# One masked product over 128 rows in a gated recurrence, and its operations ordered behind the weight splits of their steps

## The chip, the cores and the metric

The kernel runs on one core of a Trainium2 chip. The metric is the time of one execution on the device in microseconds. A profile is a trace of one execution, with each engine's instructions: TensorE (PE, with its weight loads PEld), VectorE (DVE), ScalarE (ACT), GpSimd (POOL), SyncE (SP) and the DMA queues.

## What is computed

The reference is two layers of a decoder trunk over 256 tokens of width 2048. Layer 0 has a mixer with two halves: chunked spatial gating (A) and a gated linear recurrence with 8 heads of width 128 (B). Layer 1 has an attention with 16 heads. Each layer ends in a gated MLP with a short convolution. Only the recurrence of half B is touched by the change:

```
k = (1 - lb) * sigmoid(-f);   log_f = log(lb + (1 - lb) * sigmoid(f))
per head, per chunk of 64 tokens, with G = cumsum(log_f):
  o_t = (q_t * exp(G_t)) @ state  +  sum over s <= t of (q_t * exp(G_t - G_s) . k_s) * i_s
  state = exp(G_end) * state + sum over s of (k_s * exp(G_end - G_s)) outer i_s
o = rms_norm(o) * silu(g)
```

Everything else of the trunk is large projections: a 256 x 2048 activation times weight matrices that add up to 435 MB.

## The kernel before

**The projections.** The weights stream from memory once, in pieces of 512 KB (128 partitions by 1024 floats). `weights` loads a piece `w` through SP's queue and splits it in `halves` (lines 187 to 190) into a rounded high half `wh` by ACT (line 188) and a low half `wl` by DVE (line 189). TensorE then multiplies high by high, high by low and low by high, so that three matmuls in a lower precision stand for one in full precision. `project_four`, `project_tok` and `project` differ in which side is moved; their matmuls are lines 363 to 365, 344 to 346 and 319. One piece is one *step*: the projection calls `tick()`, then `weights`, then writes out the step's matmuls, 12 of 512 columns or 24 of 256. There are four buffers for `w` and three each for `wh` and `wl`.

**Side work.** Everything that isn't a projection is written as Python generators. `tick()` advances up to `depth[0]` of them by one `yield`, so that their operations are written out between the pieces. A planner then fixes the order on each engine: it keeps the dependencies and, where an operation that was written earlier isn't ready by its own model of time, puts a later one that is ready ahead of it. On the chip each engine follows that order. Two helpers bind the planner. `tied` keeps a matmul behind the projection matmul written last. `held` (with the anchor "wh" by default, or "wl") adds an order without a semaphore: the operation may not stand ahead of the split that was written last, the `wh` split on ACT or the `wl` split on DVE.

```
def held(r, last="wh"):

    tc.add_manual_dep(r.ins, deep[last].ins.name, order, reason="not before")
```

**The gates** (`gates`, lines 671 to 688). For two groups of four heads, six steps after their projection: four sigmoids on ACT give the forget gates `l` and the two key tiles in `t` (lines 679 to 682; the trace puts them on line 100, in the helper `act`), and DVE scales the keys (line 685). Only the first sigmoid of a head is held.

**The recurrence** (`hgrn`, lines 716 to 818). A head starts at least `PACE` = 4 steps after the head before, and goes by `yield`s:
- Step 1: ACT turns `l` into the decay (line 723). DVE inverts a half of it into `kd` (line 727), ACT copies keys into `kd` (line 728), POOL multiplies them (lines 729 and 731) and forms the running products `tot` of the levels 2 to 64 (line 737).
- Step 2: eight small matmuls (line 742) of 32 rows and 32 columns each give the pairs of neighbouring tokens, two for each of the four 32-row blocks. Their results lie in one PSUM tile `dg`, 128 rows by 2 x 32 columns. Then DVE multiplies them with the mask `two` into the diagonal blocks of the state tile `st` (128 rows by 2 x 128 columns): four products of 32 rows by 64 elements, one for each block (line 745).
- Steps 3 to 5: seven levels; for each, ACT copies two halves into `E` (line 757), and DVE multiplies queries and keys with the decay (line 761, or 764 at the last one).
- Five steps on: the matmuls of the levels (lines 771 and 779), ACT's copies (lines 782 and 784), DVE's five masked copies into `st[:, 1]` (line 790), and ACT's copy to `s1` (line 793).
- Some five steps on: the output matmuls with the values (lines 801 to 803) and their evacuation (lines 805 and 809).

`sts` are four state tiles that the heads take in turn. They are set to zero once (line 709); only the blocks that line 745 writes, and the places that lines 784 and 790 write, change afterwards.

While the eight heads go through, the projections of the queries (`project`, line 864), of the values (`project_tok`, line 823) and of the output gate (`project_four`, line 869) run on TensorE.

Of the kernel before, what the change touches and what calls it, by code (L numbers as in the profile page):

```python
# [12 lines left out]
ALU = mybir.AluOpType  # L13
# [42 lines left out]
def tile_trunk(ctx: ExitStack, tc: tile.TileContext, x, pp_d, cst_d, mlev_d, msk_d,  # L56
# [36 lines left out]
    def act(out_, in_, func, **kw):  # L93
        name = TABLE.get(func)
        if name is not None and name != epoch["set"]:
            ld = SC.preload_act_table_set(name)
            for o in epoch["ops"]:
                tc.add_manual_dep(ld.ins, o.ins.name, order, reason="table order")
            epoch.update(set=name, load=ld, ops=[ld])
        r = SC.activation(out_, in_, func, **kw)  # L100
        if name is not None:
            tc.add_manual_dep(r.ins, epoch["load"].ins.name, order, reason="table order")
            epoch["ops"].append(r)
        return r
# [403 lines left out]
    def mixer_ab(norm):  # L508
# [162 lines left out]
        def gates(j, z):  # L671

            for _ in range(LAG):
                yield
            for i in range(4):
                l = keep("lf")
                t = hp.tile([P, 4, P], F32, tag="two", name=nm("kq"), bufs=2 * NH)
                first, second = view(z, i * S, (2, P)), view(z, (i + 1) * S - 1, (-2, P))
                held(act(l[:, 0:P], first, AF.Sigmoid))
                act(l[:, P:S], second, AF.Sigmoid)  # L680
                act(t[:, 0], first, AF.Sigmoid, scale=-1.0)
                act(t[:, 3], second, AF.Sigmoid, scale=-1.0)
                h = len(kq)
                ks = view(t, 0, (3 * P, 2), (1, P))
                V.tensor_scalar(ks, ks, omlb[:, h:h + 1], None, ALU.mult)
                lf.append(l)
                kq.append(t)
                yield
# [16 lines left out]

        H = P // 2
        sts = [hp.tile([P, 2, P], F32, tag=f"st{i}", name=f"st{i}") for i in range(4)]
        for st in sts:
            V.memset(st, 0.0)

        within = [px.tile([P, 512], F32, tag=f"lv{i}", name=f"lv{i}") for i in range(2)]
        for w in within:
# [3 lines left out]
        def hgrn(h):  # L716
# [3 lines left out]
                yield  # L720
            first[0] = steps[0] + PACE
            yield
            SC.activation(l, l, AF.Identity, bias=lb[:, h:h + 1], scale=omlb[:, h:h + 1])
            st = sts[h % 4]
            kd = hp.tile([P, 2, P], F32, tag="kd", name=nm("kd"), bufs=1)
            later, kb = view(l, 1, (P - 1, 2), (2, H)), view(kd, 1, (P - 1, 2), (2, H))
            V.reciprocal(kb, later)
            SC.activation(view(kd, 0, (P + 1, 2), (2, H)), view(t, 0, (3 * P + 1, 2), (2, H)), AF.Copy)
            nc.gpsimd.tensor_tensor(kb, kb, view(t, 1, (3 * P - 1, 2), (2, H)), ALU.mult)
            qs = view(t, 2 * P + 1, (-P - 1, 2), (2, H))  # L730
# [9 lines left out]
            for T in range(2):  # L740
                for r in range(0, P, BLK):
                    tied(PE.matmul(dg[r:r + BLK, T * BLK:(T + 1) * BLK], kd[:, T, r:r + BLK], t[:, 2 - T, r:r + BLK],
                                   start=True, stop=True))
            for r in range(0, P, BLK):
                V.tensor_tensor(st[r:r + BLK, :, r:r + BLK], dg[r:r + BLK, 0:2 * BLK].rearrange("p (a b) -> p a b", a=2),
                                two[r:r + BLK, :, r:r + BLK], ALU.mult)
            yield

            qs = view(t, 2 * P, (1 - P, 2), (2, H))
            V.tensor_tensor(qs, qs, view(l, 0, (P + 1, 2), (2, H)), ALU.mult)  # L750
            E = hp.tile([P, NL - 1, 2, P], F32, tag="E", name=nm("E"), bufs=2)
            for li in reversed(range(NL)):
                n = LEVELS[li]
                m = P // n
                for sl in range(2 if n > 1 else 0):
                    to = P + n if sl else 3 * P + n
                    SC.activation(E[:, li, sl].rearrange("p (b two n) -> p b two n", two=2, n=n),
                                  view(t, P * sl, (2 * n, 64 // n), (to, 2), (1, n)), AF.Copy)
                if li:
                    both = view(t, 0, (2 * P + n, 2), (2 * n, P // n), (1, n))  # L760
                    V.tensor_tensor(both, both, view(tot[n], 1, (-1, 2), (2, m), (0, n)), ALU.mult)  # L761
                else:
                    even = view(t, 0, (P, 2), (1, n))
                    V.tensor_tensor(even, even, view(tot[n], 1, (m, 2), (0, n)), ALU.mult)
                if n in (4, 16):
                    yield
# [12 lines left out]
                    deep["last"] = tied(PE.matmul(d[r:r + BLK, c:c + n], E[:, li, 0, r:r + BLK], E[:, li, 1, o:o + n],  # L779
                                                  start=True, stop=True))  # L780
            s128 = hp.tile([P, P], F32, tag="s128", name=nm("s128"), bufs=3)
            SC.activation(back(s128), xps[:, 0:P], AF.Copy)
            for r in (0, H):
                SC.activation(st[r:r + H, r // H, H - r:P - r], xps[r:r + H, P:P + H], AF.Copy)
            for li in reversed(range(1, NL - 1)):

                n = LEVELS[li]
                d, c = places[li]
                sv = view(st[:, 1], 0, (2 * n, 64 // n), (n - P, 2), (1, n))
                V.copy_predicated(sv, *(t_.rearrange("p (b two n) -> p b two n", two=2, n=n)  # L790
                                        for t_ in (msk[:, li * P:(li + 1) * P], d[:, c:c + P])))
            s1 = hp.tile([P, P], F32, tag="s1", name=nm("s1"), bufs=2)
            SC.activation(back(s1), st[:, 1], AF.Copy)
            for _ in range(5 + (h < NH - 1)):
# [7 lines left out]
            tied(PE.matmul(op[:, P:S], s128, i0, start=True, stop=False))  # L802
            tied(PE.matmul(op[:, P:S], s1, i1, start=False, stop=True))
            o = os_[h // 4]
            SC.activation(o[:, :, d0:d0 + P], op[:, 0:S].rearrange("p (t d) -> p t d", t=2), AF.Copy)
            so = sos[:, h // 4]
            ot = op[:, S:S + P]
            for T in range(2):
# [658 lines left out]
```

## Time and profile before

| | |
|---|---|
| median of the runs before | 2179.85 us (lowest 2176.77) |
| the profiled execution | 2178.03 us, of which its span from first to last instruction is 2176.2 us |
| PE busy, DVE busy, ACT busy, POOL busy | 2166.6, 1602.5, 1310.5, 473.9 us |
| weights read | 435.24 MB, 201 GB/s over the span |
| first and last small matmul of the recurrence's step 2 (line 742) | 103.9 and 199.0 us |

Each row of a view stands for one instruction or a group: line, engine, operation, what it writes `<-` what it reads, shapes. A number behind `x` counts instructions; in the grouped view the busy microseconds and the mean nanoseconds of one follow, then the engine's idle time just before them and what ended it. In the view of waits a row reads: who waited, for whom, microseconds in all, times, the longest. In the timeline a row starts with its start and its length in microseconds, and a bracket gives the idle time of the engine before it. TensorE's matmuls overlap in a pipeline, and their ends are modelled: a matmul's 0.38 us is longer than the distance to the next one.

### The profile page before, as it was taken

What the parts mean: (1) busy time and instruction counts of PE and PEld (TensorE: products, weight loads), DVE (VectorE), ACT (ScalarE), POOL (GpSimd) and SP (SyncE); (2) the same over time, 40 slices, a digit from 0 to 9 for tenths busy, and PEclk for the clock granted to TensorE, in tenths of its full rate; (3) what the DMA queues carried; (4) which work ended last, traced back from release to release, by engine and by line L of the source; (5) the groups of instructions that cost most, each with busy time, mean ns of one, the idle gap of its engine ahead of it and who ended that gap; (6) DMA issues with size and microseconds to landing.
All of it is one profiled execution on the core that took longest, in us unless ns stands there. A gap on an engine that the chain in (4) does not pass through costs nothing.

```text
span 2176.2 us, 32617 instructions
## 1 busy us (share of the span) xinstructions
PE 2166.6 (100%) x10874; PEld 1900.5 (87%) x10874; DVE 1602.5 (74%) x2294; ACT 1310.5 (60%) x1951; POOL 473.9 (22%) x865
## 2 busy tenths in 40 slices
PE   9999999999999999999999999999999999999999
PEld 8988888888888888888888888888888888888888
DVE  7788768777567757776887787877777577667766
ACT  6777766666556545654565566766666466456642
POOL 1352222212012002111133544222211012011202
PEclk9999999999999999999999999999999999999999
DMA  8755687878677767776767767787777677766866
GB/s 296 216 159 175 196 248 222 251 221 245 210 225 213 231 210 217 228 236 207 231 229 225 222 218 216 218 239 242 227 229 242 197 232 217 229 213 199 255 215 189
DMA packets 492617, 483.62 MB, mean 222 GB/s; under 512 B 115136, under 2 KB 460240, under 8 KB 492320
## 3 DMA queue, kind: packets, MB, share of 16 engines
q1 hardware_dynamic: 465888, 453.27, 66.5%
q0 software_dynamic: 24832, 25.92, 5.1%
q10 hardware_dynamic: 1728, 2.35, 0.4%
q8 instruction: 85, 1.39, 0.3%
q14 instruction: 84, 0.69, 0.1%
HBM read 435.24 MB, written 2.11 MB: 201 GB/s over the span
## 4 chain that ended last, share of the span: by engine, by line
PE 87%; DVE 5%; ACT 3%; DMA 2%; issue 2%; SPq 1%; DVEq 0%; ACTq 0%
PE pm L364 24%; PE pm L363 24%; PE pm L365 24%; PE pm L344 3%; PE pm L345 3%; PE pm L346 3%; DVE wl L189 1%; ACT wh L188 1%; SPq L383 1%; DMA w<-in_w_up 1%; PE pm L239 1%; PE pm L319 1%; PE pm L263 1%; DVE kq L761 0%; DVE tmp L376 0%
## 5 line engine op out<-in xcount | busy, mean ns | idle before, releaser
L189 DVE TENSOR_TENSOR wl<-w,wh 128x1024 fp32r<-128x1024 f32 (+1 forms) x820 | 990.7, 1219 | 437.8 <-ACT wh L188 426.0
L188 ACT ACTIVATE wh<-w 128x1024 fp32r<-128x1024 f32 (+1 forms) x820 | 855.7, 1049 | 598.9 <-PE pm L365 421.6
L364 PE MATMUL pm<-wl,a 128*128 128x512 f32 x1728 | 655.5, 379 | 0.9 <-DVE wl L189 0.8
L363 PE MATMUL pm<-wh,a 128*128 128x512 f32 x1728 | 655.8, 379 | 0.0
L365 PE MATMUL pm<-wh,a 128*128 128x512 f32 x1728 | 654.9, 379 | 0.0
L383 POOL DMA_DIRECT2D zt<-tmp x413 | 224.3, 551 | 1134.3 <-DVE tmp L376 1047.7
L364 PEld LDWEIGHTS pm<-wl,a 128*128 128x128 f32 x1728 | 326.6, 189 | 49.0 <-DVE wl L189 3.2
L363 PEld LDWEIGHTS pm<-wh,a 128*128 128x128 f32 x1728 | 326.6, 189 | 46.4
L365 PEld LDWEIGHTS pm<-wh,a 128*128 128x128 f32 x1728 | 326.6, 189 | 46.1
L363 PE MATMUL pm<-wh,hid 128*128 128x512 f32 x688 | 260.8, 379 | 0.0
L364 PE MATMUL pm<-wl,hid 128*128 128x512 f32 x688 | 260.8, 379 | 0.0
L365 PE MATMUL pm<-wh,hid 128*128 128x512 f32 x688 | 260.8, 379 | 0.0
L345 PE MATMUL pm<-wl,a 128*128 128x512 f32 x416 | 158.3, 381 | 2.1 <-DVE wl L189 2.0
L344 PE MATMUL pm<-wh,a 128*128 128x512 f32 x416 | 158.7, 381 | 0.4 <-ACT a L401 0.4
L346 PE MATMUL pm<-wh,a 128*128 128x512 f32 x416 | 157.8, 379 | 0.0
L364 PEld LDWEIGHTS pm<-wl,hid 128*128 128x128 f32 x688 | 130.0, 189 | 18.5
L363 PEld LDWEIGHTS pm<-wh,hid 128*128 128x128 f32 x688 | 130.0, 189 | 18.5
L365 PEld LDWEIGHTS pm<-wh,hid 128*128 128x128 f32 x688 | 130.0, 189 | 18.4
L1273 ACT ACTIVATE conv<-zt,pp 128x256 f32<-128x256 f32 x176 | 95.8, 589 | 74.6 <-DMA zt<-tmp 62.5
L383 POOL DMA_DIRECT2D turn<-tmp x160 | 87.2, 553 | 225.7 <-DVE tmp L376 155.3
L1274 DVE SCALAR_TENSOR_TENSOR conv<-zt,pp,conv 128x255 f32<-128x255 f32 x176 | 80.1, 479 | 57.5 <-ACT conv L1273 37.2
L376 DVE STREAM_TRANSPOSE tmp<-z 128x512 f32<-128x512 f32 x120 | 98.4, 857 | 6.4 <-ACT z L1259 5.3
(254 smaller groups left out, 2217.1 us busy)
## 6 DMA issues: line engine op xcount, KB each, us to landing
w<-in_w_up SPq DMA_DIRECT2D x352, 512.0 KB, 4.9
w<-in_w_dn SPq DMA_DIRECT2D x176, 512.0 KB, 4.9
w<-in_w_cqkv SPq DMA_DIRECT2D x96, 512.0 KB, 4.7
w<-in_w_abo SPq DMA_DIRECT2D x32, 512.0 KB, 5.0
w<-in_w_cg SPq DMA_DIRECT2D x32, 512.0 KB, 4.7
w<-in_w_co SPq DMA_DIRECT2D x32, 512.0 KB, 4.8
zt<-tmp SPq DMA_DIRECT2D x414, 32.0 KB, 2.6
zt<-tmp POOLq DMA_DIRECT2D x413, 32.0 KB, 2.5
```

The costliest lines, as they stand in the source:

```text
L188: r = deep["wh"] = SC.activation(wh, w, AF.Copy)
L189: deep["wl"] = V.tensor_tensor(wl, w, wh.bitcast(F32), ALU.subtract)
L344: PE.matmul(to_two(ps[T]), ah, h, start=k + i == 0, stop=False)
L345: PE.matmul(to_two(ps[T]), ah, l, start=False, stop=False)
L346: deep["last"] = PE.matmul(to_two(ps[T]), al, h, start=False, stop=k + i == KT - 1)
L363: PE.matmul(to_rows(ps[T]), ah, h, start=not begun and k + i == ks[0], stop=False)
L364: PE.matmul(to_rows(ps[T]), ah, l, start=False, stop=False)
L365: deep["mm"] = deep["last"] = PE.matmul(to_rows(ps[T]), al, h, start=False, stop=not more and k + i == ks[-1] + 1)
L376: V.transpose(tmp.rearrange("p (b m i t) -> p b m i t", b=4, m=4, t=2)[:, :, :, :, T], src(T).rearrange("p (m b j) -> p b m j", m=4, b=4))
L383: queues[(a + b) % len(queues)].dma_start(dst[BLK * b:BLK * (b + 1), :, a * n:(a + 1) * n], tmp[BLK * a:BLK * (a + 1), b * 4 * n:(b + 1) * ...
L1273: held(SC.activation(c, z, AF.Identity, bias=pp[:, cb:cb + 1], scale=w(2)))
L1274: V.scalar_tensor_tensor(c[:, 1:], z[:, :S - 1], w(1), c[:, 1:], ALU.mult, ALU.add)
```

## The change

- The four products of 32 rows by 64 elements become one product of 128 rows by 256: the PSUM tile `dg` is read four times over (a stride of zero over the blocks), and the mask `two`, which is zero outside the diagonal blocks, writes the rest of the state tile to zero. So the zeroing of the four state tiles at the start is gone.
- `held` is put around the other three sigmoids and the scaling in `gates`, and in `hgrn` around ACT's lines 723, 757, 782 and 805 and DVE's lines 727, 745, 750, 761 and 790.

Nothing changes in the matmuls, in the shapes of the other operations, or in what is loaded.

```diff
@@ gates
                 held(act(l[:, 0:P], first, AF.Sigmoid))
-                act(l[:, P:S], second, AF.Sigmoid)
-                act(t[:, 0], first, AF.Sigmoid, scale=-1.0)
-                act(t[:, 3], second, AF.Sigmoid, scale=-1.0)
+                held(act(l[:, P:S], second, AF.Sigmoid))
+                held(act(t[:, 0], first, AF.Sigmoid, scale=-1.0))
+                held(act(t[:, 3], second, AF.Sigmoid, scale=-1.0))
...
-                V.tensor_scalar(ks, ks, omlb[:, h:h + 1], None, ALU.mult)
+                held(V.tensor_scalar(ks, ks, omlb[:, h:h + 1], None, ALU.mult), "wl")
@@ mixer_ab
         sts = [hp.tile([P, 2, P], F32, tag=f"st{i}", name=f"st{i}") for i in range(4)]
-        for st in sts:
-            V.memset(st, 0.0)
@@ hgrn
-            SC.activation(l, l, AF.Identity, bias=lb[:, h:h + 1], scale=omlb[:, h:h + 1])
+            held(SC.activation(l, l, AF.Identity, bias=lb[:, h:h + 1], scale=omlb[:, h:h + 1]))
...
-            V.reciprocal(kb, later)
+            held(V.reciprocal(kb, later), "wl")
...
-            for r in range(0, P, BLK):
-                V.tensor_tensor(st[r:r + BLK, :, r:r + BLK], dg[r:r + BLK, 0:2 * BLK].rearrange("p (a b) -> p a b", a=2),
-                                two[r:r + BLK, :, r:r + BLK], ALU.mult)
+            held(V.tensor_tensor(st.rearrange("p a (b c) -> p a b c", c=BLK), view(dg, 0, (BLK, 2), (0, P // BLK), (1, BLK)),
+                                 two.rearrange("p a (b c) -> p a b c", c=BLK), ALU.mult), "wl")
             yield
 
             qs = view(t, 2 * P, (1 - P, 2), (2, H))
-            V.tensor_tensor(qs, qs, view(l, 0, (P + 1, 2), (2, H)), ALU.mult)
+            held(V.tensor_tensor(qs, qs, view(l, 0, (P + 1, 2), (2, H)), ALU.mult), "wl")
...
-                    SC.activation(E[:, li, sl].rearrange("p (b two n) -> p b two n", two=2, n=n),
-                                  view(t, P * sl, (2 * n, 64 // n), (to, 2), (1, n)), AF.Copy)
+                    held(SC.activation(E[:, li, sl].rearrange("p (b two n) -> p b two n", two=2, n=n),
+                                       view(t, P * sl, (2 * n, 64 // n), (to, 2), (1, n)), AF.Copy))
...
-                    V.tensor_tensor(both, both, view(tot[n], 1, (-1, 2), (2, m), (0, n)), ALU.mult)
+                    held(V.tensor_tensor(both, both, view(tot[n], 1, (-1, 2), (2, m), (0, n)), ALU.mult), "wl")
...
-            SC.activation(back(s128), xps[:, 0:P], AF.Copy)
+            held(SC.activation(back(s128), xps[:, 0:P], AF.Copy))
...
-                V.copy_predicated(sv, *(t_.rearrange("p (b two n) -> p b two n", two=2, n=n)
-                                        for t_ in (msk[:, li * P:(li + 1) * P], d[:, c:c + P])))
+                held(V.copy_predicated(sv, *(t_.rearrange("p (b two n) -> p b two n", two=2, n=n)
+                                             for t_ in (msk[:, li * P:(li + 1) * P], d[:, c:c + P]))), "wl")
...
-            SC.activation(o[:, :, d0:d0 + P], op[:, 0:S].rearrange("p (t d) -> p t d", t=2), AF.Copy)
+            held(SC.activation(o[:, :, d0:d0 + P], op[:, 0:S].rearrange("p (t d) -> p t d", t=2), AF.Copy))
```

## The prediction, made before the change was run

> **What bounds the kernel now.** I read the page first: the busy shares, the granted clock, and the chain that ended last.
>
> ```profile
> span 2176.2 us, 32617 instructions
> ...
> PE 2166.6 (100%) x10874; PEld 1900.5 (87%) x10874; DVE 1602.5 (74%) x2294; ACT 1310.5 (60%) x1951; POOL 473.9 (22%) x865
> ...
> PEclk9999999999999999999999999999999999999999
> ...
> PE 87%; DVE 5%; ACT 3%; DMA 2%; issue 2%; SPq 1%; DVEq 0%; ACTq 0%
> ```
>
> TensorE is busy for 2166.6 of 2176.2 us at full clock, and 87% of the chain runs through it. So side work on DVE and ACT costs time only where TensorE waits for it, and the most that any such change can win is what TensorE now waits. Next I read the stretches: the recurrence (about 90 to 212 us) beside an equally long one after it.
>
> ```profile
> core 0: us, PE busy (x) PEld busy (x) DVE busy (x) ACT busy (x) POOL busy (x), PEclk, DMA share, GB/s
> 90.00:212.00 122.00, 118.91 (x1194) 107.66 (x1193) 101.06 (x197) 87.41 (x240) 49.50 (x89) 1.00 0.58 174
> 212.00:334.00 122.00, 121.94 (x616) 106.41 (x615) 87.93 (x116) 84.35 (x120) 30.46 (x56) 1.00 0.74 219
> ```
>
> In the recurrence TensorE is idle for 122.00 - 118.91 = 3.09 us, after it for 0.06 us. DVE is the fuller of the two helpers (101.06 of 122, 83%). Then the waits of this stretch:
>
> ```profile
> ACT E L757 <- DVE kq L761: 16.9, 19, 2.1
> DVE wl L189 <- ACT wh L188: 8.6, 16, 1.6
> ...
> ACT s L793 <- DVE st L790: 5.7, 4, 2.3
> ...
> PE pm L345 <- DVE wl L189: 2.0, 4, 0.8
> ...
> PE pm L319 <- DVE wl L189: 0.4, 2, 0.3
> PE px L742 <- POOL kq L731: 0.4, 1, 0.4
> ...
> PE px L742 <- DVE mg L585: 0.2, 1, 0.2
> ```
>
> TensorE waits six times for a late low half (2.0 + 0.4 us) and twice for the inputs of the small matmuls (0.6 us). A wait costs more than its row says, as one of the six shows in the timeline of TensorE:
>
> ```profile
> 135.07 0.38 PE L344 MATMUL pm<-wh,a 128*128 128x512 f32 x1
> ...
> 136.18 0.48 PE L345 MATMUL pm<-wl,a 128*128 128x512 f32 x1 [0.73 <-DVE wl L189]
> ...
> 136.50 0.38 PE L346 MATMUL pm<-wh,a 128*128 128x512 f32 x1
> ...
> 136.71 0.38 PE L344 MATMUL pm<-wh,a 128*128 128x512 f32 x1
> ```
>
> Undisturbed matmuls follow each other at 0.21 us (136.50 to 136.71). Here the next comes 1.11 us after the one at 135.07, and the one behind it 0.32 us later: 0.90 + 0.11 = 1.0 us lost where the row says 0.73, about 0.27 more. The six waits therefore cost an estimated 2.4 + 6 x 0.27 = 4.0 us. That is all that faster splits can win here, 0.2% of the kernel.
>
> **Part 1: one product for four.** Why was the low half late at 136.18? DVE's timeline ahead of it:
>
> ```profile
> 128.97 1.41 DVE L189 TENSOR_TENSOR wl<-w,wh 128x1024 fp32r<-128x1024 f32 x1
> ...
> 131.06 0.25 DVE L745 TENSOR_TENSOR st<-px,pairs 32x64 f32<-32x64 f32 x1
> 131.29 0.30 DVE L790 COPY_PREDICATED st<-msk,lv 128x128 f32<-128x128 uint16 x1
> 131.63 0.22 DVE L745 TENSOR_TENSOR st<-px,pairs 32x64 f32<-32x64 f32 x1
> 131.88 0.30 DVE L790 COPY_PREDICATED st<-msk,lv 128x128 f32<-128x128 uint16 x1
> ...
> 133.72 0.94 DVE L727 RECIPROCAL kd<-lf 128x128 f32<-128x128 f32 x1
> ...
> 134.91 1.21 DVE L189 TENSOR_TENSOR wl<-w,wh 128x1024 fp32r<-128x1024 f32 x1
> ```
>
> Between two splits DVE does over 4 us of recurrence, the four products among it. One product holds DVE for 0.25 us (131.63 to 131.88), so four take 1.0 us. The trace has no 128x256 product of this kind; the rows around it are these:
>
> ```profile
> L189 DVE TENSOR_TENSOR wl<-w,wh 128x1024 fp32r<-128x1024 f32 x39 | 49.2, 1264 | 8.7 <-ACT wh L188 8.6
> ...
> L745 DVE TENSOR_TENSOR st<-px,pairs 32x64 f32<-32x64 f32 x32 | 7.1, 221 | 0.5
> ...
> L585 DVE SCALAR_TENSOR_TENSOR mg<-px,pp,wt 128x256 f32<-128x256 f32 x8 | 3.5, 477 | 0.0
> ```
>
> ```profile
> L1361 DVE TENSOR_TENSOR y<-y,pm 128x512 f32<-128x512 f32 x8 | 5.2, 680 | 0.0
> ```
>
> From 64 elements (221 ns) to 512 (680 ns) a product grows by 1.02 ns an element, which gives 0.42 us for 256; line 585, as large and with one input from PSUM too, takes 0.48. I take 0.45, between these near ends. So a head saves 1.0 - 0.45 = 0.55 us of DVE, eight heads 4.4 us. Had all 32 partitions' pieces cost only their own busy time (4 x 0.221), the saving would be 0.43.
>
> (The Trainium skill, "VectorE: DVE Perf Modes", section "The TRN2 errata", counts 120 cycles at 0.96 GHz plus one an element for an operation from PSUM: an estimate of 0.39 us for the one and 0.19 for each of the four. The row of 0.221 is above that, so I stay with the rows; by the page the saving would be about 0.6 us a head.)
>
> How much of it reaches TensorE? At most 0.55 us in each of the six waits, 3.3 us; nothing if no product lies ahead of the late split. There are eight products among the 39 splits of this stretch. I take four of the six waits as relieved: **-2.2 us** (ends 0 and -3.3).
>
> **Part 2: the zeroing that goes.**
>
> ```profile
> 1.01 1.09 DVE L709 MEMSET st<- 128x256 f32 x4
> ...
> 4.16 0.35 DVE L403 TENSOR_SCALAR a<-x,pp 128x256 fp32r<-128x256 f32 x1 [0.92 <-DMA x<-in_x]
> ```
>
> DVE loses 1.09 us of work at the start, but waits 0.92 us for the first load anyway. Cost and gain 0: the load hides it. Without that cover the gain would be 1.09 us.
>
> **Part 3: the orders.** `held` forbids one thing only, to stand ahead of the split written last. Which operations stand ahead of theirs now? The decay (line 723) and the inversion (line 727) are written a line or two apart, in step 1 of the same head:
>
> ```profile
> L723 ACT ACTIVATE lf<-lf,gm x8: 583/586/600, 83.6 to 116.5; 128x256 f32<-128x256 f32 x8
> ...
> L727 DVE RECIPROCAL kd<-lf x8: 939/944/976, 86.8 to 188.8; 128x128 f32<-128x128 f32 x8
> ```
>
> All eight decays are done by 117 us, while the last inversion comes at 188.8: the planner has pulled the decays far ahead. `held` puts each back into its head's first step, behind a `wh` split. That adds 0.59 us to ACT there, ahead of the inversion, the running products on POOL, and whatever ACT does next: a split, or the evacuation of line 784 for which DVE's line 790 waits. What may hide it is ACT's own idle time: it waits 16.9 + 5.7 us for DVE in this stretch. Against that, DVE waited for a `wh` in 16 of its 39 splits. If every decay pushed the chain, it would cost 8 x 0.586 = 4.7 us; if it fell into idle time each time, 0. TensorE waited at 6 of 39 splits, which is 1.2 in eight; a decay lies close to the next split, so I take more, two of eight: **+1.2 us**.
>
> The sigmoids and the scaling move by a few steps at most, at 79 to 113 us:
>
> ```profile
> L100 ACT ACTIVATE lf<-turn 128x128 f32<-128x128 f32 x16 | 4.8, 330 | 4.1 <-DMA turn<-tmp 4.1
> ...
> L100 ACT ACTIVATE kq<-turn 128x128 f32<-128x128 f32 x16 | 4.0, 316 | 0.0
> ```
>
> They now stand ahead of splits for which they could make TensorE wait; behind them, three (0.95 us) come later in each of eight steps, and the eight scalings on DVE with them. Their users are the heads, the last of which start long after. I take 0; should the cover be gone (a head waiting for its gates), it is 0.95 us a head, 7.6 us. They also waited 4.1 us for a load, with what was queued behind them on ACT; the split no longer stands there, so a small gain isn't excluded, up to the 0.2 us that line 742 waited for line 585 on DVE. The other held operations (lines 745, 750, 761, 790 on DVE; 757, 782, 805 on ACT) depend on matmuls, copies or products of their own step. I expect none ahead of its split, so that `held` binds nothing: 0. No DMA moves, and SP's queue is passed by nothing.
>
> **Sum.** -2.2 + 1.2 = -1.0 us, against the profiled execution's own 2178.03 us (its span of 2176.2 and 1.8 around it): **2177.0 us**. Its place to the runs: 2178.03 lies between the lowest (2176.77) and the median (2179.85). With the ends of the terms, and orders elsewhere that the planner may choose anew, its own range is 2174 to 2180. The kernel has 9.6 us of idle TensorE in all (2176.2 - 2166.6), 6.5 of it outside this stretch, which bounds what such new orders can win.
>
> **The rivals.**
> - *Nothing arrives (2178.0).* The change saves DVE time, but ACT is the link that ends last: the pair of lines 757 and 761 alternates, and DVE waits 8.6 us for `wh`. For it: most of the eight products may lie in steps where TensorE doesn't wait at all (it waits at 6 of 39). Against it: at 136.18 DVE did not wait for ACT, it was simply full.
> - *Slower (2182.7).* The decay delays `wh` or line 784 in every head: 8 x 0.586 = 4.7 us, and the saving on DVE then lies in time in which DVE waits for ACT. It decides when the decay falls where ACT has no idle time before the next split. In these two rows ACT stood idle and the split behind went only after it:
>
> ```profile
> 171.89 0.54 ACT L757 ACTIVATE E<-kq 128x128 f32<-128x128 f32 x2 [1.31 <-POOL tot L737]
> 172.33 1.04 ACT L188 ACTIVATE wh<-w 128x1024 fp32r<-128x1024 f32 x1
> ```
>
>   (The Trainium skill, "Perfetto Trace Analysis", section "Per-engine timelines", says that ACT, DVE and GpSimd take instructions strictly in order; by that an operation moved in front of a split always delays it by its whole length, unless the engine was idle. The trace agrees: the split at 172.33 went behind line 757's wait of 1.31 us.) Against it: the inversion at 133.72 stands behind DVE's own work with no wait ahead of it, so the decay has room before it is the last input.
> - *The whole wait goes (2173.4).* The relief of DVE clears all six waits and the two of line 742: 4.0 + 0.6 us. It needs the decays to cost nothing, and every late split to owe less than 0.55 us to DVE; the one of 136.18 owes 1.0, which speaks against it.
>
> **How the numbers follow.** Forecast 0.5, nothing 0.2, slower 0.2, the whole wait 0.1. The range reaches from beyond the last to beyond the third, with some 3 us on each side for orders elsewhere: 2170 to 2186. All four cases lie within 2% (44 us, about what a measurement of this kernel can tell from no change). To leave that, TensorE would have to wait over 1 us more at each of the 39 splits, or win five times its idle time: faster 0.01, same 0.97, slower 0.02.
>
> **What would show it.** Line 745 x8 at 0.42 to 0.48 us; no line 709; line 723 spread from about 91 to 192 us; TensorE's wait for `wl` between 90 and 212 us down from 2.4 to about 1.5 us; line 745's busy time lower by about 3.5 us (7.1 to 3.6). Wrong if TensorE's idle time in the stretch rises above 4 us (the third rival), if it falls under 1 us (the fourth), or if the time leaves 2174 to 2180 by waits outside this stretch.

## The result and the profile after

| | before | after |
|---|---|---|
| median of 20 runs each | 2178.84 us | 2175.22 us |
| lowest | 2176.77 us | 2171.63 us |
| ratio of times, 95% interval | | 0.9981 [0.9975, 0.9987] |

The changed kernel is faster by 0.19%, or 4.1 us [2.8, 5.4]. That lies inside both ranges of the prediction, but the forecast was a gain of 1.0 us. Three of these 40 executions were disturbed (2838 us before, 10219 and 3855 us after) and don't enter the ratio; the one that was profiled after is among them, so the profile after is that of the same kernel in the run e1_after (first experiment). The page of after, its head:

```profile
span 2172.1 us, 32592 instructions
...
PE 2164.4 (100%) x10874; PEld 1900.6 (87%) x10874; DVE 1597.0 (74%) x2266; ACT 1309.2 (60%) x1951; POOL 469.9 (22%) x865
```

TensorE's instructions are the same, in the same order but for two small matmuls of the levels, which stand a few places earlier. DVE has 28 instructions fewer: 24 products (three in each of eight heads) and the four zeroings. The span is 4.1 us shorter. The view by stretches of after:

```profile
core 0: us, PE busy (x) PEld busy (x) DVE busy (x) ACT busy (x) POOL busy (x), PEclk, DMA share, GB/s
90.00:212.00 122.00, 121.18 (x1211) 111.05 (x1210) 99.69 (x177) 92.26 (x252) 51.98 (x98) 1.00 0.58 178
212.00:334.00 122.00, 121.94 (x616) 106.57 (x615) 89.12 (x120) 82.86 (x116) 30.33 (x56) 1.00 0.74 224
```

In the recurrence TensorE is now idle for 122.00 - 121.18 = 0.82 us instead of 3.09; the equally long stretch behind it is as it was. The waits of TensorE in that stretch, after:

```profile
PE pm L345 <- DVE wl L189: 0.5, 2, 0.4
PE px L740 <- POOL kq L729: 0.3, 1, 0.3
```

Two of six waits for a low half are left, and one of the two for the small matmuls (line 742 before is line 740 here). The lines that were to show the parts, in after (line, engine, operation, shortest/median/longest in ns, first and last start in us):

```profile
L742 DVE TENSOR_TENSOR st<-px,pairs x8: 411/418/454, 105.6 to 196.8; 128x256 f32<-128x256 f32 x8
```

```profile
L721 ACT ACTIVATE lf<-lf,gm x8: 588/600/611, 91.0 to 187.3; 128x256 f32<-128x256 f32 x8
```

The product takes 0.418 us, and the decays, which all ran before 117 us, are spread up to 187.3.

**A marker for the stage.** Idle time in a window of fixed ends misses waits that leave the window. A better measure is when the projection behind the recurrence starts: TensorE does the same work up to there. In the tile `yb`, before and after:

```profile
L363 PE MATMUL pm<-wh,yb x64: 379/379/379, 281.5 to 353.4; 128*128 128x512 f32 x64
```

```profile
L363 PE MATMUL pm<-wh,yb x64: 379/379/379, 277.5 to 349.4; 128*128 128x512 f32 x64
```

281.5 against 277.5: the marker comes 4.0 us earlier. It counts from the span's start, though, and so takes in what happens ahead of the stage. The projection of the queries (line 319), with which the stage begins, starts at another time in every profile, between 88.8 and 89.5 us, and TensorE waits for nothing between 60 us and there, so that the difference comes from the first 60 us, ahead of every order and product. Before, after, e4 and e9 (experiments below):

```profile
89.29 0.61 PE L319 MATMUL pm<-a,wh 128*128 128x256 f32 x4
```

```profile
89.19 0.61 PE L319 MATMUL pm<-a,wh 128*128 128x256 f32 x4
```

```profile
89.36 0.39 PE L319 MATMUL pm<-a,wh 128*128 128x256 f32 x2
```

```profile
88.80 0.61 PE L319 MATMUL pm<-a,wh 128*128 128x256 f32 x4
```

So the text goes by the *stage*, from this start to the marker: 192.2 us before and 188.3 after, 3.9 us less, which is the whole gain in time. The stage is also clearer than the time. Later in the kernel TensorE has a few waits for `wl` that differ between profiles, although the order of the instructions on every engine is that of before from 212 us on. The 1050 us that begin 768.5 us behind the marker show it, here in the two runs at the ends, e4 and e6 (PE busy is the second number):

```profile
1044.80:2094.80 1050.00, 1049.36 (x4968) 1.00 0.73 226
```

```profile
1046.30:2096.30 1050.00, 1046.25 (x4946) 1.00 0.73 225
```

TensorE is idle there for 0.64 us in e4 and for 3.75 in e6; before has 1.27 in the same stretch, after 1.87. In a single execution this shifts the time by 1 or 2 us, and a ratio of times leaves differences of 1 us open. So marker and stage are set beside it. Each is from one execution, and differences of 0.3 us in the stage aren't told apart here.

### The profile page after: what moved, and what is told of

The parts are those of the page before. It is cut to its first block, busy times and chain, and to the rows that moved or that the text cites. A ratio compares the mean times of both kernels' runs of the same rounds, so it can differ in the third digit from the quotient of the medians.

```text
span 10217.7 us, 32592 instructions
## 1 busy us (share of the span) xinstructions
PE 10213.2 (100%) x10874; PEld 6495.0 (64%) x10874; DVE 1599.1 (16%) x2266; ACT 1311.4 (13%) x1951; POOL 459.1 (4%) x865
## 4 chain that ended last, share of the span: by engine, by line
PE 100%; DVE 0%; issue 0%
PE pm L363 27%; PE pm L364 27%; PE pm L365 27%; PE pm L344 4%; PE pm L346 4%; PE pm L345 4%; PE pm L319 3%; PE pm L239 2%; PE pm L263 1%; PE px L582 0%; PE px L1049 0%; PE px L1102 0%; PE lv L776 0%; PE px L1099 0%; PE px L1046 0%; PE px L798 0%
## 5 line engine op out<-in xcount | busy, mean ns | idle before, releaser
L363 PE MATMUL pm<-wh,a 128*128 128x512 f32 x1728 | 2399.2, 1388 | 0.0
L365 PE MATMUL pm<-wh,a 128*128 128x512 f32 x1728 | 2396.8, 1387 | 0.0
L364 PE MATMUL pm<-wl,a 128*128 128x512 f32 x1728 | 2396.4, 1387 | 0.0
L363 PEld LDWEIGHTS pm<-wh,a 128*128 128x128 f32 x1728 | 1157.2, 670 | 669.7 <-issue 669.2
L364 PEld LDWEIGHTS pm<-wl,a 128*128 128x128 f32 x1728 | 1158.1, 670 | 666.8 <-issue 666.8
L365 PEld LDWEIGHTS pm<-wh,a 128*128 128x128 f32 x1728 | 1145.2, 663 | 669.7 <-issue 669.6
L363 PE MATMUL pm<-wh,hid 128*128 128x512 f32 x688 | 875.6, 1273 | 0.0
L364 PE MATMUL pm<-wl,hid 128*128 128x512 f32 x688 | 875.3, 1272 | 0.0
L365 PE MATMUL pm<-wh,hid 128*128 128x512 f32 x688 | 875.1, 1272 | 0.0
L363 PEld LDWEIGHTS pm<-wh,hid 128*128 128x128 f32 x688 | 397.7, 578 | 266.8 <-issue 266.8
L364 PEld LDWEIGHTS pm<-wl,hid 128*128 128x128 f32 x688 | 395.7, 575 | 265.0 <-issue 265.0
L365 PEld LDWEIGHTS pm<-wh,hid 128*128 128x128 f32 x688 | 392.3, 570 | 265.7 <-issue 265.7
L344 PE MATMUL pm<-wh,a 128*128 128x512 f32 x416 | 479.8, 1153 | 0.0
L345 PE MATMUL pm<-wl,a 128*128 128x512 f32 x416 | 479.8, 1153 | 0.0
L346 PE MATMUL pm<-wh,a 128*128 128x512 f32 x416 | 479.2, 1152 | 0.0
L346 PEld LDWEIGHTS pm<-wh,a 128*128 128x128 f32 x416 | 197.9, 476 | 157.4 <-issue 156.8
L344 PEld LDWEIGHTS pm<-wh,a 128*128 128x128 f32 x416 | 198.1, 476 | 153.9 <-issue 152.9
L345 PEld LDWEIGHTS pm<-wl,a 128*128 128x128 f32 x416 | 198.8, 478 | 151.2 <-issue 151.2
L319 PE MATMUL pm<-a,wh 128*128 128x256 f32 x256 | 196.6, 1058 | 0.0
```

What stands on the lines that cost most here:

```text
L319: deep["last"] = PE.matmul(to_tokens(ps), t[:, k * P:(k + 1) * P], by_tokens(acts[done + k], o), start=done + k + o == 0 and t is wh, stop ...
L344: PE.matmul(to_two(ps[T]), ah, h, start=k + i == 0, stop=False)
L345: PE.matmul(to_two(ps[T]), ah, l, start=False, stop=False)
L346: deep["last"] = PE.matmul(to_two(ps[T]), al, h, start=False, stop=k + i == KT - 1)
L363: PE.matmul(to_rows(ps[T]), ah, h, start=not begun and k + i == ks[0], stop=False)
L364: PE.matmul(to_rows(ps[T]), ah, l, start=False, stop=False)
```

## The experiments

The theories were these. The first: the gain is DVE's, from the product, larger than costed, and the decay's order takes some back. The rival: the gain is the orders', which keep recurrence work from standing ahead of a split, and the product changes little. Each run was timed beside the kernel before; the time in us is the ratio applied to the median of before that was taken with it (2177.28 us for e1 to e4, 2178.82 for e5 to e8, 2178.49 for e9 to e12). The stage is the difference of the two starts, with its distance from before in brackets.

| run | edit | time, us | ratio [95%] | marker, us | stage, us | idle TensorE 90 to 212, us |
|---|---|---|---|---|---|---|
| before | | | | 281.5 | 192.2 | 3.09 |
| e1 | the whole change | -4.4 | 0.9980 [0.9971, 0.9989] | 277.5 (-4.0) | 188.3 (-3.9) | 0.82 |
| e2 | product alone | -2.6 | 0.9988 [0.9979, 0.9996] | 277.3 (-4.2) | 188.0 (-4.2) | 0.55 |
| e3 | orders alone | -0.2 | 0.9999 [0.9990, 1.0008] | 281.2 (-0.3) | 192.2 (0.0) | 2.57 |
| e4 | the change, decay free | -6.3 | 0.9971 [0.9960, 0.9983] | 276.3 (-5.2) | 186.9 (-5.3) | 0.00 |
| e5 | product, gates' orders | -6.3 | 0.9971 [0.9960, 0.9983] | 275.9 (-5.6) | 187.1 (-5.1) | 0.00 |
| e6 | product, inversion's order | -4.8 | 0.9978 [0.9969, 0.9987] | 277.8 (-3.7) | 188.4 (-3.8) | 0.86 |
| e7 | four products of 128 rows | -3.9 | 0.9982 [0.9973, 0.9991] | 279.2 (-2.3) | 189.7 (-2.5) | 1.68 |
| e8 | four products done twice | +5.2 | 1.0024 [1.0015, 1.0034] | 286.7 (+5.2) | 197.5 (+5.3) | 8.35 |
| e9 | the change, decay in the gates | -5.0 | 0.9977 [0.9968, 0.9985] | 275.7 (-5.8) | 186.9 (-5.3) | 0.00 |
| e10 | product, gates' orders of heads 0 to 3 | -4.4 | 0.9980 [0.9971, 0.9989] | 277.3 (-4.2) | 188.3 (-3.9) | 0.69 |
| e11 | product, gates' orders of heads 4 to 7 | -5.0 | 0.9977 [0.9966, 0.9987] | 276.2 (-5.3) | 187.1 (-5.1) | 0.00 |
| e12 | gates' orders alone | -1.1 | 0.9995 [0.9987, 1.0004] | 280.5 (-1.0) | 191.0 (-1.2) | 2.40 |

### e1: the whole change, again

The edit is the diff above, unchanged.

> The changed kernel itself, for a profile of an undisturbed execution and a time beside its parts. Both theories: 3 to 5 us faster than before (about 2175). In the profile, between 90 and 212 us, TensorE's wait for the low half (wl) falls from 2.4 to under 1.5 us; line 742's one product takes 0.42 to 0.48 us.

Measured: -4.4 us, stage -3.9. It repeats the result and gives the profile.

### e2: the product alone

Before, with one product and no zeroing; no order is added.

```
-            for r in range(0, P, BLK):
-                V.tensor_tensor(st[r:r + BLK, :, r:r + BLK], dg[r:r + BLK, 0:2 * BLK].rearrange("p (a b) -> p a b", a=2),
-                                two[r:r + BLK, :, r:r + BLK], ALU.mult)
+            V.tensor_tensor(st.rearrange("p a (b c) -> p a b c", c=BLK), view(dg, 0, (BLK, 2), (0, P // BLK), (1, BLK)),
+                            two.rearrange("p a (b c) -> p a b c", c=BLK), ALU.mult)
```

> Only the one product for four, without the zeroing; no new held. Theory 1 (the product gives the gain, 0.55 us of DVE in each head, and the decays' return to their steps costs about 1 us): 1 us faster than the whole change, 2174, 4 to 5 us under before. Theory 2 (the orders give the gain, the product lies in time that DVE has): within 1 us of before, 2178.

Measured: stage -4.2 us, time -2.6 [-4.6, -0.9]. In the stage the product alone gives as much as the whole change.

### e3: the orders alone

After, with the four products (each held) and the zeroing back.

```
-            held(V.tensor_tensor(st.rearrange("p a (b c) -> p a b c", c=BLK), view(dg, 0, (BLK, 2), (0, P // BLK), (1, BLK)),
...
+            for r in range(0, P, BLK):
+                held(V.tensor_tensor(st[r:r + BLK, :, r:r + BLK], dg[r:r + BLK, 0:2 * BLK].rearrange("p (a b) -> p a b", a=2),
+                                two[r:r + BLK, :, r:r + BLK], ALU.mult), "wl")
```

> Only the orders: every new held, the four products kept (each held) and the zeroing kept. Theory 1: within 1 us of before or 1 to 2 us slower, 2179 to 2181. Theory 2: most of the gain, 2175 to 2176.

Measured: -0.2 us [-2.2, +1.7], stage 0.0. The orders together are worth nothing that was measured. The rival falls as it was put; but e4 shows that this nothing is a sum.

### e4: the change without the decay's order

```
-            held(SC.activation(l, l, AF.Identity, bias=lb[:, h:h + 1], scale=omlb[:, h:h + 1]))
+            SC.activation(l, l, AF.Identity, bias=lb[:, h:h + 1], scale=omlb[:, h:h + 1])
```

> The whole change, but the decay (ACT's Identity on the gates, the operation that was pulled 4 to 23 steps ahead) without held. Theory 1 with the decay's price of 1.2 us: 1 us faster than the whole change, 2174. Theory 2, if the decays are what gains: 2 to 4 us slower than the whole change. If the decay falls into ACT's idle time: the same as the whole change within 0.7 us.

Measured: -6.3 us, stage 186.9 against 188.3 us with the order. The decay's order costs 1.4 us. A part of how it does so stands in the waits of POOL between 90 and 212 us, first after, then e4:

```profile
POOL tot L735 <- ACT lf L721: 29.9, 6, 11.6
...
POOL kd L727 <- ACT kd L726: 8.3, 4, 4.1
```

```profile
POOL kd L727 <- ACT kd L726: 29.3, 6, 11.4
```

In after POOL waits six times for the decay before it can start the running products of a head (line 735), work that it did early before. In the last head this goes on to TensorE. ACT, POOL and TensorE of after:

```profile
187.28 0.59 ACT L721 ACTIVATE lf<-lf,gm 128x256 f32<-128x256 f32 x1
```

```profile
187.95 0.50 POOL L735 TENSOR_TENSOR tot<-lf 128x128 f32<-128x128 f32 x1 [11.61 <-ACT lf L721]
188.53 2.66 POOL L735 TENSOR_TENSOR tot<-tot 128x64 f32<-128x64 f32 x5
193.64 0.73 POOL L727 TENSOR_TENSOR kd<-kd,kq 128x128 f32<-128x128 f32 x1 [2.45 <-ACT kd L726]
194.44 0.51 POOL L729 TENSOR_TENSOR kq<-kq,lf 128x128 f32<-128x128 f32 x1
```

```profile
195.01 0.33 PE L740 MATMUL px<-kq,kd 128*32 128x32 f32 x16 [0.28 <-POOL kq L729]
```

The decay comes at 187.28, POOL has waited 11.61 us for it, its products end at 194.95, and TensorE's small matmuls, which need them, wait 0.28 us. The two waits for `wl` of after (at 134.97 and 172.79 us) are gone in e4 too; its TensorE waits for nothing in the stretch. DVE has no idle time ahead of these two low halves (they begin at 133.54 and 171.32 us), so the `wh` of their own piece isn't what they came late by. How the decay's order leads to them wasn't separated.

### e5 and e6: which orders gain

e4 is faster than the product alone by the stage (186.9 against 188.0), so one of the other orders gains. Two candidates are the gates (the three sigmoids and the scaling) and the inversion; each was added to e2.

```
+                held(act(l[:, P:S], second, AF.Sigmoid))
+                held(act(t[:, 0], first, AF.Sigmoid, scale=-1.0))
+                held(act(t[:, 3], second, AF.Sigmoid, scale=-1.0))
...
+                held(V.tensor_scalar(ks, ks, omlb[:, h:h + 1], None, ALU.mult), "wl")
```

> The one product, and of the orders only the gates' (three sigmoids and the scaling of each head); decay and inversion free. Marker: the first matmul that reads yb (before 281.5 us, product alone 277.3, whole change without the decay's hold 276.3). Theory G (the gates' operations stood in front of splits): 276.3, 2171 to 2172 us. Theory I (the two inversions that stood ahead are what gains): 277.3, 2174 us.

```
+            held(V.reciprocal(kb, later), "wl")
```

> The one product, and of the orders only the inversion's. Theory G: marker at 277.3 us, 2174 us, as the product alone. Theory I: 276.3, 2171 to 2172 us.

Measured: e5's stage is 187.1 us, 0.9 shorter than that of e2, with no wait of TensorE left; e6's is 188.4, no gain. The gates' orders gain, the inversion's doesn't. (By the marker e5 seemed to gain 1.4 us; 0.5 of that lies ahead of the stage, which begins at 88.8 us in e5 and at 89.3 in e2.)

### e7 and e8: is it the number of products or their length?

e7 keeps four products and lets each go over all 128 rows by 64 elements (the mask is zero off the diagonal); e8 does the four products of before twice, the second time with the same values.

```
-                V.tensor_tensor(st[r:r + BLK, :, r:r + BLK], dg[r:r + BLK, 0:2 * BLK].rearrange("p (a b) -> p a b", a=2),
-                                two[r:r + BLK, :, r:r + BLK], ALU.mult)
+                V.tensor_tensor(st[:, :, r:r + BLK], dg[:, 0:2 * BLK].rearrange("p (a b) -> p a b", a=2),
+                                two[:, :, r:r + BLK], ALU.mult)
```

> Four products as before, but each over 128 rows and the 64 elements of one block's columns; no zeroing; no new orders. The order on every engine is that of before. Theory C (the number of products costs, not their rows): 0.22 us each at a pitch of 0.25, marker 281.5, time that of before within 1 us. Theory Q (a piece that begins in another group of 32 rows must wait for the one ahead of it, which one start for all spares): pitch 0.15, 3 us of DVE less, marker 279 to 280.

```
-            for r in range(0, P, BLK):
+            for r in range(0, 2 * P, BLK):
+                r %= P
```

> The kernel before with the four products written twice over (the same values again): 1.0 us more of DVE in each head. Theory 1 (DVE's time in these steps reaches TensorE, as 5.4 us less on DVE brought 4.2): marker 6 to 8 us later, 288, 2184 us. Rival (the gain of the one product comes from the planner's other order, not from DVE's time): marker within 2 us of 281.5.

Measured, e8: +5.2 us in time and marker, less than the 6 to 8 expected, but far from the rival's 2. One more set, some 1.0 us of DVE in each of eight heads, costs 5.3 of 8 us in the stage. So DVE's time works in both directions. The planner's order differs in e8 as well as in e2, so that the two by themselves don't exclude a gain by another order. e7 does: in its trace the instructions of every engine stand in the order of before, only the four zeroings are missing.

Measured, e7: the stage is 2.5 us shorter than before, with as many products of the same length and none of the orders. The group of the products in e7:

```profile
L743 DVE TENSOR_TENSOR st<-px,pairs x32: 215/216/258, 107.5 to 198.8; 128x64 f32<-128x64 f32 x32
```

0.216 us as against 0.222 before: their own time can't be it. DVE's timeline of e7, at the place that the prediction showed for before:

```profile
130.86 0.25 DVE L743 TENSOR_TENSOR st<-px,pairs 128x64 f32<-128x64 f32 x1
131.10 0.31 DVE L788 COPY_PREDICATED st<-msk,lv 128x128 f32<-128x128 uint16 x1
131.30 0.22 DVE L743 TENSOR_TENSOR st<-px,pairs 128x64 f32<-128x64 f32 x1
131.44 0.30 DVE L788 COPY_PREDICATED st<-msk,lv 128x128 f32<-128x128 uint16 x1
131.64 0.22 DVE L743 TENSOR_TENSOR st<-px,pairs 128x64 f32<-128x64 f32 x1
```

In e7 a pair of copy and product takes 0.34 us (131.30 to 131.64), before it took 0.57 (131.06 to 131.63). Before, the product started when the copy ahead had ended (131.29 + 0.30 = 131.59, then 131.63). In e7 it starts 0.11 us ahead of that end (131.10 + 0.31 = 131.41, but 131.30), and the copy behind a product 0.08 us ahead of the product's end (131.30 + 0.22 = 131.52, but 131.44). The rows that a product covers are what differs: their number, or where they start. Before itself tells which, since its first product has 32 rows too but begins at row 0, as the copies do. The copy ahead of it:

```profile
130.82 0.45 DVE L790 COPY_PREDICATED st<-msk,lv 128x128 f32<-128x128 uint16 x1
```

That copy ends at 131.27, and the first product starts at 131.06, 0.21 us ahead (0.20 in the head at 157.63); the other three, from rows 32, 64 and 96, start 0.03 to 0.04 us behind the end of theirs. So it is the first row. Where the four stand in a row, the same shows, in before and then in e7:

```profile
106.96 0.91 DVE L745 TENSOR_TENSOR st<-px,pairs 32x64 f32<-32x64 f32 x4
107.90 0.34 DVE L750 TENSOR_TENSOR kq<-kq,lf 128x128 f32<-128x128 f32 x1
```

```profile
107.51 0.61 DVE L743 TENSOR_TENSOR st<-px,pairs 128x64 f32<-128x64 f32 x4
108.03 0.32 DVE L748 TENSOR_TENSOR kq<-kq,lf 128x128 f32<-128x128 f32 x1
```

From the first product to what follows them, before takes 0.94 us and e7 0.52. The Trainium skill, "VectorE: DVE Perf Modes", section "Two Vector instructions with no wait between them", has a rule for it, which it calls a model: an instruction that has an input or an output in another quadrant of 32 partitions than the last instruction that read, or wrote, the same memory starts only when every earlier Vector instruction has finished. The trace agrees: pieces that begin at rows 32, 64 and 96 between copies that begin at row 0 cost 0.23 us more a pair than pieces with a common start.

### e9: the decay held, but early

If the price of the decay's order is that it comes late, it must vanish when the decay is written earlier, in the gates, and held there.

```
+                held(SC.activation(l, l, AF.Identity, bias=lb[:, h:h + 1], scale=omlb[:, h:h + 1]))
                 lf.append(l)
...
-            held(SC.activation(l, l, AF.Identity, bias=lb[:, h:h + 1], scale=omlb[:, h:h + 1]))
```

> The whole change, but the decay is written (and held) in the gates, behind the head's sigmoids, instead of in the recurrence's first step. Marker as before (whole change 277.5 us, decay free 276.3). Theory L (the decay's price is that it comes in a full step of the recurrence, in front of ACT's splits and POOL's running products): marker 276 to 276.5, 2171 to 2172 us. Theory H (any hold of the decay costs): 277.5, 2173 us or more.

Measured: no idle TensorE, and a stage of 186.9 us: 1.4 us shorter than with the order in the heads, and as long as without one. So it is the lateness that costs and not the hold. (Its marker is 0.6 us earlier than e4's because its stage begins 0.56 us earlier, 88.80 against 89.36.) In time e9 has -5.0 [-7.0, -3.3], which doesn't separate it from the change itself: its TensorE is idle for 3.22 us in the 1050 us far behind the marker, where e4 has 0.64. The profiled execution of e9 lies at the median of its runs (2174.36 and 2174.16 us), so whether this later idle time is the kernel's or the execution's stays open.

### e10, e11 and e12: where the gates gain

e10 adds the gates' orders to e2 for the first four heads only, e11 for the last four; e12 adds them all to before, with its four products.

```
+            def keep_step(r, last):
+                if j == 0:
+                    held(r, last)
```

(With `j == 1` in e11.)

> The one product, and the gates' orders for the first four heads alone (their gates run at 79 to 88 us). Product alone: marker 277.3; product with all gates' orders: 275.9. Theory N (the sigmoids of the second four, at 100 to 113 us, stood in front of splits of the recurrence): 277.3. Theory P (what gains is the other order that the planner makes of the whole stage): not told apart by the times of the gates, between 275.9 and 277.3 or beyond.

> The one product, and the gates' orders for the last four heads alone. Theory N: marker 275.9. Theory P: anywhere between 275.9 and 277.3 or beyond.

> Four products as before, and only the gates' orders. If product and gates add up: marker 281.5 - 1.4 = 280.1, 1 to 2 us faster than before. If the gates' orders gain only where the product has made room: 281.5, time of before.

Measured by the stage: e10 188.3 us, no gain on e2 (188.0); e11 187.1, 0.9 us shorter; e12 191.0, 1.2 shorter than before. The gain comes from the orders of the second four heads, whose gates run at 100 to 113 us, where the recurrence has begun, and doesn't need the one product. The low halves at that place, e2 and then e11, in DVE's timeline:

```profile
101.19 1.23 DVE L189 TENSOR_TENSOR wl<-w,wh 128x1024 fp32r<-128x1024 f32 x1 [0.59 <-ACT wh L188]
...
104.38 1.23 DVE L189 TENSOR_TENSOR wl<-w,wh 128x1024 fp32r<-128x1024 f32 x1 [0.39 <-ACT wh L188]
```

```profile
100.05 1.23 DVE L189 TENSOR_TENSOR wl<-w,wh 128x1024 fp32r<-128x1024 f32 x1 [1.56 <-ACT wh L188]
...
103.62 1.22 DVE L189 TENSOR_TENSOR wl<-w,wh 128x1024 fp32r<-128x1024 f32 x1 [1.30 <-ACT wh L188]
```

With the orders these splits come 1.14 and 0.76 us earlier, and DVE waits longer for ACT ahead of them. But this lead is lost again: two splits on they start at 111.45 us in e2 and 111.42 in e11, and another two on at 117.22 and 117.52. The next two, e2 and then e11:

```profile
120.67 1.23 DVE L189 TENSOR_TENSOR wl<-w,wh 128x1024 fp32r<-128x1024 f32 x1 [0.40 <-ACT wh L188]
...
123.75 1.57 DVE L189 TENSOR_TENSOR wl<-w,wh 128x1024 fp32r<-128x1024 f32 x1 [0.49 <-ACT wh L188]
```

```profile
120.35 1.16 DVE L189 TENSOR_TENSOR wl<-w,wh 128x1024 fp32r<-128x1024 f32 x1
...
121.87 1.21 DVE L189 TENSOR_TENSOR wl<-w,wh 128x1024 fp32r<-128x1024 f32 x1
```

Here e11 comes 1.88 us ahead: the planner has put a split in front of recurrence work that stands ahead of it in e2. The order on DVE, ACT and POOL differs between the two runs in several such places up to 145 us. So the gates' orders act, in part at least, through the order that the planner makes of the stage behind them; by which place they clear the waits at 135 and 173 us wasn't separated and stays open.

## Why the prediction was right or wrong

The measured gain (3.6 us by the medians, 4.1 by the ratio) came in a stage whose waits the prediction had bounded at 4.0 + 0.6. The place was right, and the bound nearly. The sum of -1.0 us fell short of it by 3 us for two reasons: the product was costed at 2.2 us and won 4.2, and the gates' orders were put at nothing. That the time lies in the prediction's ranges is owed to their width.

1. **What bounds the kernel: right.** The gain came where TensorE waited for low halves between 90 and 212 us, and the idle time of the stretch went from 3.09 to 0.82 us. The estimate that a wait costs 0.27 us more than its row says was of the right size: five of the eight waits in the view went, the idle time fell by 2.27 us and the stage by 3.9, which is 0.3 us more for each. The bound of 4.6 us was a little low, since the estimate wasn't applied to the two waits of line 742: in e4 and e9, where every wait is gone, the stage won 5.3 us.

2. **Part 1, one product, -2.2: right mechanism, size too small.** The product alone made the stage 4.2 us shorter (time -2.6 [-4.6, -0.9]). The smaller fault is "a head saves 1.0 - 0.45 = 0.55 us". The 1.0 us was near (four in a row take 0.94), and the length of the one product was nearly right (0.418 for 0.45), but its length isn't what it costs, since the next instruction starts before it ends. DVE's timeline of after:

```profile
128.40 0.41 DVE L742 TENSOR_TENSOR st<-px,pairs 128x256 f32<-128x256 f32 x1
128.73 0.33 DVE L747 TENSOR_TENSOR kq<-kq,lf 128x128 f32<-128x128 f32 x1
```

   From start to start it is 0.33 us, so that a head saves 0.94 - 0.33 = 0.61 to 1.0 - 0.33 = 0.67 us, some 5 in eight. The prediction mixed two measures: a pitch (131.63 to 131.88) for the old products, a busy time for the new one. (The 0.6 us that it sets beside this mixes them too: 4 x 0.19 - 0.39 would be 0.37.) It also had the four at 4 x 0.221 as the alternative and didn't ask why their pitch was larger than their length. e7 gives the answer, their different first rows; that alone is worth 2.5 of the 4.2 us, with the order of every engine as before. The other 1.7 came with the one product in place of the four; its pitch is shorter (0.33 us against the 0.52 of e7's four), but the planner's order differs in e2 too, and the two weren't separated.

   The larger fault is the step "four of the six waits as relieved", at 0.55 us each. In e2 two waits are left with 0.5 us, and both of line 742 are gone too: six of eight went, and the idle time fell by 2.54 us. With the extra 0.27 us for each that the prediction had found itself, and counted in its bound but not in its -2.2, this makes 2.54 + 6 x 0.27 = 4.2 us, which is what the stage won, more than the 3.3 named as the most that the product could.

3. **Part 2, the zeroing, 0: right.** The first DVE instruction that needs a load waits longer for it, 1.93 us for 0.92, and starts at 4.07 for 4.16:

```profile
4.07 0.35 DVE L403 TENSOR_SCALAR a<-x,pp 128x256 fp32r<-128x256 f32 x1 [1.93 <-DMA x<-in_x]
```

   The load hides it, as the sum had it: TensorE's stage begins at 89.19 us for 89.29, less than this start differs between other profiles.

4. **Part 3, the decay, +1.2: right in size, and by luck in part.** By the stage it costs 1.4 us (188.3 against 186.9). The way is in part another than the one named. The prediction took it as two of eight decays that push a split on ACT. The runs show POOL waiting for the decay (29.9 us in six waits), and its running products late for the small matmuls at 195.01, which accounts for one of the three waits that are gone in e4. POOL was named as a user, but not costed. The other two waits are for `wl`, with DVE full ahead of them; a split held up on ACT wasn't shown for them.

5. **Part 3, the gates, 0: wrong.** "I take 0", with a small gain up to 0.2 us left open; they gain 0.9 (e5, e11) to 1.2 us (e12). The prediction priced what comes later (0.95 us a head) and asked when its users start; to the splits that come earlier it gave at most the 0.2 us that line 742 waited. Those at 100 to 105 us do come earlier, though the lead lasts only to 111 us. What it left out of the sum is that a few operations held back make the planner order the stage behind them anew; it had named that for its range alone.

6. **Part 3, the other orders, 0: right** for the inversion (e6). For the rest, e4 and e5 differ only by those and the inversion's, and are 0.2 us apart in the stage with the same ratio of times, 0.9971.

**The sum by the stage:** -4.2 (product), -0.9 to -1.2 (gates) and +1.4 (decay) give -3.7 to -4.0 us; measured -3.9. Without the product: +0.2 to +0.5; e3 has 0.0. The terms add up within what single executions can show.

**The rivals.** The idle time of the stretch fell under 1 us, which the prediction had named as the sign that its forecast was wrong and "the whole wait goes" (2173.4, a gain of 4.6) was right. The stage's -3.9 is nearer to that rival, which had a chance of 0.1, than to the forecast, though three waits are left. The reason given against it, that the split of 136.18 owes 1.0 us to DVE, holds in so far as that wait isn't gone. It is the same piece, TensorE in after:

```profile
134.97 0.48 PE L345 MATMUL pm<-wl,a 128*128 128x512 f32 x1 [0.19 <-DVE wl L189]
```

It has 0.19 us left of 0.73. "Nothing arrives" and "slower" fell; the decay's price is real, though, and is the 1.4 us that e4 gets back.

**A better version.** e4 and e5, without the decay's order, are faster than before (0.9971). The change has 0.9980 in e1; the intervals overlap, so in time the lead over the change isn't sure. In the stage they win 5.3 and 5.1 us for the change's 3.9. e9, which holds the decay early, has the stage of e4; its time doesn't tell it from the others.

## What to carry to other kernels

When short instructions of one engine are merged, count both sides from start to start; where the pitch of the old ones is larger than their length, ask what keeps them apart before costing the new one. Keep the pieces of a tile on the same first partition where VectorE works back to back, even if most of the extra rows are masked away. An order that holds work back is judged operation by operation: here one group of four gained and one operation lost about as much, so that together they looked like nothing. A marker that counts from the start of the program takes in the start's own scatter: measure a stage from its own first instruction.

## What was not expected of the hardware

- VectorE overlapped neighbouring instructions by about 0.1 us (0.41 us long, the next after 0.33; a product 0.11 us ahead of the end of a copy), but not where a piece began at another row than the instruction ahead (rows 32, 64, 96 against 0): a pair of copy and product took 0.57 us with pieces of 32 rows and 0.34 us with pieces of 128 rows by as many elements. A common first row isn't enough by itself: the copies of one head that follow each other all begin at row 0 and write the same tile, and they start 0.03 us behind the end of the one ahead (198.67 + 0.30 us, the next at 199.00, in before).
- More rows cost VectorE nothing in this product: 0.216 us for 128 rows by 64 elements, 0.222 for 32 by 64.
